# A group of seven in the first feed-forward and packed score products, in a conformer trunk on one Trainium2 core

## Chip, core and metric

The kernel runs on one core of one Trainium2 chip. The metric is the device time of one launch in microseconds (us). Engines are named as the profile names them: PE is TensorE (PEld its weight loads), DVE VectorE, ACT ScalarE, POOL GpSimd, SP SyncE, whose queue issues most of the DMAs.

## The reference

A trunk of two layers over 256 positions of width 1024, all in float32. Cut to what matters here:

```python
def swiglu_ffn(h, w1, w3, w2):                       # D_FF = 2816
    return (silu(h @ w1) * (h @ w3)) @ w2

for i in range(2):
    h = h + 0.5 * swiglu_ffn(rmsnorm(h, ffn_norm1[i]), ffn1_w1[i], ffn1_w3[i], ffn1_w2[i])
    m = rmsnorm(h, mix_norm[i])
    h = h + (conv_module(m, ...) if i == 0 else mla(m, positions, ...))
    h = h + 0.5 * swiglu_ffn(rmsnorm(h, ffn_norm2[i]), ffn2_w1[i], ffn2_w3[i], ffn2_w2[i])
return rmsnorm(h, final_norm)
```

In `mla` (8 heads) a score is the sum of two products, one over 128 unrotated components and one over 64 rotated ones, with one rotated key for all heads:

```python
q_rope, k_rope = apply_rope(q_rope, cos, sin), apply_rope(k_rope, cos, sin)   # angles from positions
for blk in range(2):                                 # query blocks of 128
    s = (einsum("bqhd,bkhd->bhqk", q_nope[:, q0:q1], k_nope[:, :q1])
         + einsum("bqhr,bkr->bhqk", q_rope[:, q0:q1], k_rope[:, :q1])) * scale
    p = softmax(where(chunk mask, s, -inf))
    o = einsum("bhqk,bkhd->bqhd", p, v[:, :q1])
```

## The kernel before

Weights come as blocks of 1 MB (128 x 2048 numbers) on SP's queue into four `raw` buffers. A block is split in two halves of 1024 columns: ACT casts it to a high part of type fp32r, DVE subtracts that from the raw numbers and keeps the low part (`load`, L246 and L247). High and low parts lie in five pairs of buffers. Activations are split in the same way (`Xh`, `Xl`), and `mm3` makes each product of three fp32r matmuls: low by high, high by high, high by low (L332, L335, L336).

A feed-forward has six chunks c of its hidden columns, each of four blocks, the last one of two. A plain block gives 24 matmuls with 512 columns. In `SEVEN_UP` stand the chunks that are worked as a *group of seven*: the four blocks are taken as a two-by-two matrix of blocks, and seven products of sums (12 matmuls each) take the place of four plain blocks of 24. `load_seven` fetches the four raws, makes sums of them in place on DVE (L200, 128 x 2048) and splits the seven results; `whole_rows` adds the activations' two parts to one tile `xs`, which takes a `raw` buffer; `sums_of_rows` and `forms_of` make four sums of it and split these; `seven_products` issues the products. The feed-forwards 1, 2 and 3 do this for chunk 3, and all four do it for part of the down product (`SEVEN_DOWN`). The feed-forwards are numbered 0 to 3; the convolution stands between 0 and 1, the attention between 2 and 3.

The gate rows of a chunk are turned by way of DRAM (`gt`, `gd`, `gb`) and split on ACT and DVE into `Gh` and `Gl` (L853). `diagonals` is a generator for work off the path that `beside()` advances. `rope_tables` makes sines and cosines of the positions; it stands in the program ahead of `mla`, and the scheduler has its DVE part in the first feed-forward, among L1366 to L1391.

In the attention `scores` puts for each head and each query block one fp32 product of `QN` and `KN` (L1584) and one of `QR` and `KR` (L1585) into the same bank. `QR` and `KR` hold the turned part of a head on one half of the partitions; rows of the other half carry the chunk mask as a product. `softmax`, `probs`, `values` and `evicted` follow, and `nope` makes the unrotated queries of heads 4 to 7 in between.

A scheduler sets the order on each engine by its own estimate of times; `order(a, b)` forces a behind b, and `urgent` gives an instruction priority.

Of the kernel before, what the change touches and what calls it, by code (L numbers as in the profile page):

```python
# [19 lines left out]
P = 128  # L20
D = 1024
S = 256
# [25 lines left out]

SEVEN_UP = {1: (3,), 2: (3,), 3: (3,)}
SEVEN_DOWN = (0, 1, 2, 3)  # L50
# [39 lines left out]
def trunk(ctx: ExitStack, tc: tile.TileContext, x, xt, first, pos, invf, gfin, wdw,  # L90
# [72 lines left out]

    casts = {}

    turns = []
# [22 lines left out]
    def load_seven(j, four, b, pieces):  # L189
# [14 lines left out]
        if j == 1:  # L204
            sub(b[11], b[12], b[11])
            sub(b[12], b[22], b[12])
        elif j == 2:
            sub(b[11], b[22], b[11])
        elif j == 6:
            sub(b[11], b[21], b[11])  # L210
# [126 lines left out]

    def sums_of_rows(x11, x12, x21, x22):


        sums = [(0, x22, x21, x22, ALU.add), (2, x21, x11, x21, ALU.subtract), (1, x11, x22, x11, ALU.subtract),
                (3, x12, x12, x11, ALU.subtract)]
        for n, out, left, right, op in sums:
            nc.vector.tensor_tensor(out, left, right, op=op)
# [23 lines left out]
    def seven_products(xh, xl, forms, banks, late={}):  # L368
# [21 lines left out]
        kept = tmp.tile([P, 512], F32, tag="s", name=uid("p5"))  # L390
        last = urgent(nc.scalar.copy)(kept, c22)
        product(forms[1], c21, False)
        add = urgent(nc.vector.tensor_add)(c12, c21, kept)
        order(casts[n0 + 5, 0][1], add.ins)
        for high, low in gates[-NT:] if not late else ():
            order(high, last.ins)
            order(low, add.ins)
        low_gates = [low for high, low in gates[-NT:] if not late]
        product(rows(1, 0), c11, False)
        product(forms[2], c21, False)  # L400
        add = urgent(nc.vector.tensor_add)(c22, c21, kept)
        order(casts[n0 + 6, 0][1], add.ins)
        for low in low_gates[1:]:
            order(low, casts[n0 + 6, PIECES - 1][1].ins)
        product(forms[3], c12, False)
# [247 lines left out]
    class Plain:  # L653
# [9 lines left out]
        @urgent  # L663
        def half(self, tb, i):
            sq = squares(self.ss[tb], h[tb], D, i)
            if tb == 0 and i == 1:
                self.sq = sq

                nc.scalar.activation(small.tile([P, 1], F32, tag="silu", name="sigm"), self.ss[0][:, 1:], AF.Sigmoid)

# [171 lines left out]
    def ffn_in(act, X, make_next, beside, apart, seven_up, seven_down):  # L842
        first_form = {}
        Gh = act.tile([P, NF, S], F32R, tag="Gh", name=uid("Gh"))
# [10 lines left out]
        def first_chunk(X, u):  # L855
# [13 lines left out]
            for n, (m, tb, ks) in enumerate(groups):  # L869
# [12 lines left out]
                last = mm  # L882

        for c in range(6):

# [4 lines left out]
            if c == 0 and X.pool:  # L890
                first_chunk(X, u)
            if seven_up and c == min(seven_up) - (1 if X.whole else 2):
                forms = forms_of(sums_of_rows(*whole_rows(X.xh, X.xl)), Gh[:, 14:], Gl[:, 14:])
            if c in seven_up:
# [4 lines left out]
                beside()  # L899
            if both and seven_down:  # L900
                z11, z21, z12, z22 = (rows4[:, n, :] for n in range(4))
                down_sums = sums_of_rows(z11, z12, z21, z22)
                first_form = forms_of(down_sums[:1], *(act.tile([P, 2, S], F32R, tag=tag, name=uid(tag))
                                                       for tag in ("s1h", "s1l")))
            for m in range(0 if u else 1 if both else 2):
# [453 lines left out]

    def rope_tables():  # L1360
        pi = const.tile([P, NT], I32, name="pi")
# [3 lines left out]
        pf = const.tile([P, NT], F32, name="pf")  # L1365
        nc.vector.tensor_copy(pf, pi)  # L1366
        ang = const.tile([P, NT, 32], F32, name="ang")
# [31 lines left out]
        nc.scalar.activation(sn[:, :, 0, :], r3, AF.Sin, scale=-1.0)  # L1399
        nc.scalar.activation(sn[:, :, 1, :], r3, AF.Sin)  # L1400
        return cc, sn

    def rope(pool, dst, src, n, cc, sn, tb, after=()):

        w = n * 64
        t1, t2 = (pool.tile([P, w], F32, tag=f"rp{w}", name=uid("rp"), bufs=3 if n > 1 else 4) for _ in range(2))
        a = t1[:, :w].rearrange("p (n i f) -> p n i f", i=2, f=32)
# [16 lines left out]
    def mla_in(act, X, make_next, cc, sn):  # L1424
# [6 lines left out]

        KR = act.tile([P, 2, S], F32, tag="KR", name="KR")
        QR = act.tile([P, 2, H // 2, S], F32, tag="QR", name="QR")
        for x, fill in ((KR, -1e30), (QR, 1.0)):
            nc.gpsimd.memset(x, 0.0)
            for parity in range(2):
                for tb in range(NT):
                    row = 64 * (1 - parity) + 32 * tb
                    t = tb * P + (CHUNK if x is KR else 0)
                    nc.gpsimd.memset(x[row:row + 1, parity, ..., t:t + CHUNK], fill)  # L1440

# [123 lines left out]
        (hi, lo), = weights()  # L1565
        for tb in range(NT):
            for d in range(2):
                b = bank("A", "v")
                for k in range(2):
                    c = slice(k * D + d * 512, k * D + d * 512 + 512)  # L1570
                    mm3(b, CKh[:, k, tbs(tb)], CKl[:, k, tbs(tb)], hi[:, c], lo[:, c], k == 0, k == 1)
                kept = nc.scalar.copy(VV[:, tb, d * 512:(d + 1) * 512], b)
# [3 lines left out]

        score_last, maxima, powers, scaled = [], [], [], []

        def scores(hd):
            b = bank("B", "sc")  # L1580
            sc = {0: b[:, :P], 1: b[:, P:P + S]}
            for qb in range(NT):
                n = (qb + 1) * P
                nc.tensor.matmul(sc[qb], QN[:, hd, tbs(qb)], KN[:, hd, :n], start=True, stop=False)  # L1584
                last = nc.tensor.matmul(sc[qb], QR[:, hd % 2, hd // 2, tbs(qb)], KR[:, hd % 2, :n], start=False,  # L1585
                                        stop=True)
            score_last.append(last)
# [21 lines left out]
        def probs(pr):  # L1609
            b = transposed(pr, 0, 3)  # L1610
            pt = act.tile([P, 3 * P], F32, tag="ptT", name=uid("ptT"), bufs=2)
            nc.scalar.copy(pt, b[:, :3 * P])
            return pt

        def evicted(hd, b):
            nc.scalar.copy(Oh[:, hd, :], b[:, :S])
            nc.vector.tensor_sub(Ol[:, hd, :], b[:, :S], Oh[:, hd, :].bitcast(F32))

        def values(hd, pt):
# [3 lines left out]

            (urgent if hd in (3, 4, 5, 6) else lambda f: f)(evicted)(hd, b)

# [4 lines left out]
        table = urgent(nc.scalar.activation)(small.tile([P, 1], F32, tag="silu", name="exp"), neghalf, AF.Exp)  # L1630
        order(table, kept.ins)
        pr[0] = scores(0)
        pr[1] = scores(1)
        pr[2] = scores(2)

        for j, i, highs, lows in ((0, 0, None, maxima[2]), (0, 1, None, scaled[0]), (1, 0, powers[2], scaled[1]),
                                  (1, 1, powers[2], scaled[2])):
            for cast, first in zip(casts[n_used[0] + j, i], (highs, lows)):
                if first is not None:
                    order(cast, first.ins)  # L1640
        nope(part, QN, 4, CQh, CQl, 512, 4, (0, 4), score_last[-1:])
        o = Rows(Oh, Ol, H)
        for i in range(2, H + 3):
# [6 lines left out]
            if i - 2 < H:  # L1650
                pt[i - 2] = probs(pr[i - 2])
            if i - 3 in pt:
                values(i - 3, pt[i - 3])
# [17 lines left out]
    def diagonals():  # L1671
# [5 lines left out]
        for g in (1, 0):  # L1677
            for j in range(KP - g):
                nc.scalar.activation(dpair[g][:, j, :], ident2, AF.Copy, scale=wp2[:, g, j:j + 1])
# [17 lines left out]

    stage = []
    todo = diagonals()

# [13 lines left out]
    X = ffn(X, lambda act: Norm("mix_1", turn_by_dma=rows), apart=True)  # L1714
    cc, sn = rope_tables()
    X = mla(X, lambda act: Norm("ffn2_1", half=True, turn_by_dma=rows), cc, sn)
# [102 lines left out]
```

## Time and profile before

| | |
|---|---|
| median of three runs | 896.05 us (895.89 to 896.4) |
| profiled execution | 896.07 us, span 894.3 us |
| granted TensorE clock | 0.999 |
| busy: PE, DVE, ACT, POOL | 99%, 83%, 64%, 12% of the span |
| DMA | 198.94 MB, 222 GB/s over the span |

The profile is one execution; starts are microseconds from the start of its span. A line of a timeline gives start, duration, engine, line, operation, output and inputs, and behind them in brackets how long the engine had been idle and what it waited for. `x24` means so many instructions in a row. TensorE's durations overlap, so its pace is read from starts. Feed-forward 0 runs to about 182 us, its chunk 3 from 71.5 us on; the scores begin at 666.3 us.

### The profile page before, as it was taken

How to read it: one execution, taken by the hardware profiler on the slowest of the kernel's cores; microseconds unless marked ns; L12 is line 12 of the kernel's file. 1: busy time of each engine (PE TensorE's matmuls, PEld its weight loads, DVE VectorE, ACT ScalarE, POOL GpSimd, SP SyncE). 2: the span in 40 equal slices, each digit the busy share in tenths (PEclk: the TensorE clock that was granted, in tenths of full speed). 3: DMA queues.
4: the chain of work that ended last, by engine and by line, in shares of the span. 5: the costliest groups of instructions: out<-in, count | busy, mean ns of one | idle time of the engine just before them, and what ended most of it. 6: DMA issues, size and time to landing. Idle time of an engine off the chain costs nothing.

```text
span 894.3 us, 12241 instructions
## 1 busy us (share of the span) xinstructions
PE 886.9 (99%) x4221; PEld 745.9 (83%) x4221; DVE 743.1 (83%) x1083; ACT 571.8 (64%) x993; POOL 104.2 (12%) x227
## 2 busy tenths in 40 slices
PE   9999999999999999999999999999999999999997
PEld 7888888898988888888888888888899888888886
DVE  6787789579998999999588989995768579989973
ACT  7966458488886646667375566673677566474752
POOL 1000000069962000000010000001400010000000
PEclk9999999999999999999999999999999999999999
DMA  9987629834215864939759369495635349378541
GB/s 330 375 303 274 232 59 355 295 121 172 106 60 194 289 258 144 374 109 388 259 175 339 118 218 357 123 392 182 223 142 189 141 154 342 104 260 317 180 196 48
DMA packets 71055, 198.94 MB, mean 222 GB/s; under 512 B 12369, under 2 KB 41937, under 8 KB 51665
## 3 DMA queue, kind: packets, MB, share of 16 engines
q1 hardware_dynamic: 70560, 197.47, 61.8%
q8 instruction: 33, 0.54, 0.2%
q10 hardware_dynamic: 432, 0.69, 0.2%
q14 instruction: 30, 0.24, 0.1%
HBM read 181.87 MB, written 16.25 MB: 222 GB/s over the span
## 4 chain that ended last, share of the span: by engine, by line
PE 92%; DVE 4%; ACT 2%; DMA 1%; issue 0%; SPq 0%; POOL 0%; DVEq 0%; ACTq 0%
PE u L336 16%; PE u L335 16%; PE u L332 16%; PE o L335 9%; PE o L336 9%; PE o L332 9%; PE gate L1005 2%; PE u L411 2%; DVE acc L1094 2%; PE u L1005 2%; PE tp L446 1%; PE a L335 1%; PE a L332 1%; PE a L336 1%; PE nope L336 1%; PE nope L332 1%
## 5 line engine op out<-in xcount | busy, mean ns | idle before, releaser
L247 DVE TENSOR_TENSOR lo<-raw,hi 128x1024 fp32r<-128x1024 f32 (+1 forms) x236 | 276.2, 1212 | 38.8 <-ACT hi L246 37.6
L246 ACT CAST hi<-raw 128x1024 fp32r<-128x1024 f32 (+1 forms) x238 | 236.8, 1044 | 89.3 <-DMA raw<-in_f2w 30.8
L332 PE MATMUL u<-lo,Xh 128*128 128x512 f32 x612 | 238.4, 389 | 0.1
L336 PE MATMUL u<-hi,Xl 128*128 128x512 f32 x612 | 238.3, 389 | 0.0
L335 PE MATMUL u<-hi,Xh 128*128 128x512 f32 x612 | 238.1, 389 | 0.0
L332 PEld LDWEIGHTS u<-lo,Xh 128*128 128x128 f32 x612 | 114.9, 188 | 24.5 <-ACT Xh L598 0.5
L336 PEld LDWEIGHTS u<-hi,Xl 128*128 128x128 f32 x612 | 114.9, 188 | 24.3 <-DVE Xl L465 0.5
L335 PEld LDWEIGHTS u<-hi,Xh 128*128 128x128 f32 x612 | 114.9, 188 | 23.8
L214 ACT CAST hi<-raw 128x1024 fp32r<-128x1024 f32 x98 | 97.7, 1050 | 51.8 <-DVE raw L200 44.9
L200 DVE TENSOR_TENSOR lo<-raw,hi 128x1024 fp32r<-128x1024 f32 x98 | 115.6, 1216 | 7.1 <-ACT hi L214 7.1
L332 PE MATMUL o<-lo,Gh 128*128 128x512 f32 (+1 forms) x276 | 106.6, 386 | 0.0
L335 PE MATMUL o<-hi,Gh 128*128 128x512 f32 (+1 forms) x276 | 106.5, 386 | 0.0
L336 PE MATMUL o<-hi,Gl 128*128 128x512 f32 (+1 forms) x276 | 106.5, 386 | 0.0
L437 POOL TENSOR_TENSOR ms<-ss 128x1 f32<-128x1 f32 x16 | 8.1, 510 | 597.6 <-ACT junk L429 597.6
L200 DVE TENSOR_TENSOR raw<-raw,raw 128x2048 f32<-128x2048 f32 x28 | 63.9, 2283 | 1.8 <-DMA raw<-in_f2w 0.9
L332 PEld LDWEIGHTS o<-lo,Gh 128*128 128x128 f32 x276 | 51.8, 188 | 10.5
L335 PEld LDWEIGHTS o<-hi,Gh 128*128 128x128 f32 x276 | 51.9, 188 | 10.5
L336 PEld LDWEIGHTS o<-hi,Gl 128*128 128x128 f32 x276 | 51.8, 188 | 10.4
L1094 DVE SCALAR_TENSOR_TENSOR acc<-V,dw,acc 128x128 f32<-128x128 f32 (+1 forms) x174 | 53.9, 391 | 0.0
L1115 ACT ACTIVATE prod<-V,dw 128x128 f32<-128x128 f32 (+1 forms) x128 | 45.6, 415 | 1.8 <-POOL Y L1116 1.0
L956 ACT ACTIVATE s<-u,R 128x512 f32<-128x512 f32 (+1 forms) x48 | 30.9, 647 | 24.8 <-PE u L336 24.1
L797 DVE SCALAR_TENSOR_TENSOR h<-o,rh,h 128x512 f32<-128x512 f32 (+1 forms) x18 | 12.9, 719 | 29.2 <-PE o L336 29.2
(265 smaller groups left out, 1257.7 us busy)
## 6 DMA issues: line engine op xcount, KB each, us to landing
raw<-in_f2w SPq DMA_DIRECT2D x66, 1024.0 KB, 6.2
raw<-in_f1w SPq DMA_DIRECT2D x62, 1024.0 KB, 6.5
raw<-in_cw SPq DMA_DIRECT2D x12, 1024.0 KB, 5.5
gd<-gt SPq DMA_DIRECT2D x160, 64.0 KB, 3.0
gb<-gd SPq DMA_DIRECT2D x24, 256.0 KB, 2.8
rows<-gd SPq DMA_DIRECT2D x16, 256.0 KB, 4.4
raw<-in_wo SPq DMA_DIRECT2D x4, 1024.0 KB, 4.9
hd<-rows SPq DMA_DIRECT2D x56, 64.0 KB, 2.4
```

What stands on the lines that cost most here:

```text
L200: ins = nc.vector.tensor_sub(out, left, right)
L214: casts[n, i] = nc.scalar.copy(hi[:, c], raw[:, c]), sub(lo[:, c], raw[:, c], hi[:, c].bitcast(F32))
L246: casts[len(loaded), i] = (nc.scalar.copy(hi[:, c], raw[:, c]), low.tensor_sub(lo[:, c], raw[:, c], hi[:, c].bitcast(F32)))
L247: low.tensor_sub(lo[:, c], raw[:, c], hi[:, c].bitcast(F32)))
L332: mm = nc.tensor.matmul(o, ah, bl, start=start, stop=False, skip_group_check=seeded)
L335: nc.tensor.matmul(o, ah, bh, start=False, stop=False, skip_group_check=seeded)
L336: return nc.tensor.matmul(o, al, bh, start=False, stop=stop, skip_group_check=seeded)
L411: mm = nc.tensor.matmul(o, al if kind == "x" else ah, bl if kind == "l" else bh, start=start and n == 0, stop=stop and n == len(kinds) - 1)
L956: nc.scalar.activation(s[:, :w], u[0, tb][:, :w], AF.Silu, scale=X.r[tb])
L1005: mm = nc.tensor.matmul(u[:, t], w[:, c], X.x[:, k, t], start=(k == 0), stop=(k == KT - 1))
L1094: dve_last.append(nc.vector.scalar_tensor_tensor(out if j == j1 - 1 else y, v, w, y, op0=ALU.mult, op1=ALU.add))
L1115: prods_last.append(nc.scalar.activation(p, v, AF.Copy, scale=w))
```

## The change

1. Chunk 3 of feed-forward 0 becomes a group of seven, like those of the other three. For all four the sums of the activations are now made two chunks ahead (before: two, or one where the feed-forward takes its input whole), behind the sixth block's low part in feed-forward 0. The sums for the group of the down product are made a little earlier in the program.
2. The turned part of the scores is made of two fp32r products. `KA` holds the high part of the turned key on both halves of the partitions, `QA` the low part of a query on one half and its high part on the other; `QR` holds the high part of the query and the mask's ones, `KR` the low part of the key and the mask. So `QA` by `KA` gives low by high and high by high, `QR` by `KR` high by low. For the second query block these two come ahead of `QN` by `KN`.
3. In `seven_products` the last two gate rows' splits stand behind the next plain block's parts, and the two before them behind one of the sums of raws.
4. `rope_tables` is made at the end of `diagonals`, so later in feed-forward 0, and the table load for the sigmoid of the convolution stands behind its last sine.
5. Around the softmax some casts of weights are put behind other instructions than before, and the eviction of head 2 gets priority too.

```diff
-SEVEN_UP = {1: (3,), 2: (3,), 3: (3,)}
+SEVEN_UP = {0: (3,), 1: (3,), 2: (3,), 3: (3,)}
...
-    def whole_rows(xh, xl):
+    def whole_rows(xh, xl, after=()):
         x = rawp.tile([P, HB], F32, tag="raw", name=uid("xs")).rearrange("p (k t) -> p k t", t=S)
-        nc.vector.tensor_add(x, xh.bitcast(F32), xl.bitcast(F32))
+        whole = nc.vector.tensor_add(x, xh.bitcast(F32), xl.bitcast(F32))
+        for a in after:
+            order(whole, a.ins)
...
+        for high, low in gates[-2 * NT:-NT] if not late else ():
+            order(low, thirds[n0 + 2].ins)
+        late_gates = []
         for high, low in gates[-NT:] if not late else ():
-            order(high, last.ins)
-            order(low, add.ins)
-        low_gates = [low for high, low in gates[-NT:] if not late]
+            late_gates.append((high, low))
...
-        for low in low_gates[1:]:
-            order(low, casts[n0 + 6, PIECES - 1][1].ins)
+        for n, (high, low) in enumerate(late_gates):
+            order(high, casts[n0 + 5 + n, PIECES - 1][0].ins)
+            order(low, casts[n0 + 7, PIECES - 1][1].ins)
...
-            if seven_up and c == min(seven_up) - (1 if X.whole else 2):
-                forms = forms_of(sums_of_rows(*whole_rows(X.xh, X.xl)), Gh[:, 14:], Gl[:, 14:])
+            if seven_up and c == min(seven_up) - 2:
+                after = [casts[5, PIECES - 1][1]] if X.whole else ()
+                forms = forms_of(sums_of_rows(*whole_rows(X.xh, X.xl, after)), Gh[:, 14:], Gl[:, 14:])
...
+            nc.scalar.copy(KA[:, tbs(t)], b[:, :P])
             for i in range(2):
                 half = slice(64 * i, 64 * i + 64)
-                nc.scalar.copy(KR[half, i, tbs(t)], b[half, :P])
+                nc.vector.tensor_sub(KR[half, i, tbs(t)], b[half, :P], KA[half, tbs(t)].bitcast(F32))
+        turns_of = [], []
         for tb in range(NT):
-            b = transposed(qr[tb], 0, 4, (last,)).rearrange("p (j t) -> p j t", t=P)
-            for parity, copy in ((0, nc.scalar.copy), (1, nc.vector.tensor_copy)):
-                half = slice(64 * parity, 64 * parity + 64)
-                urgent(copy)(QR[half, parity, :, tbs(tb)], b[half])
+            b = transposed(qr[tb], 0, 4, (last,), turns_of[tb]).rearrange("p (j t) -> p j t", t=P)
+            for parity in range(2):
+                half, rest = (slice(64 * i, 64 * i + 64) for i in (parity, 1 - parity))
+                high = QR[half, parity, :, tbs(tb)]
+                turned_last = urgent(nc.scalar.copy)(high, b[half])
+                both = act.tile([P, 512], F32R, tag="rp512", name=uid("QA"), bufs=6).rearrange("p (j t) -> p j t", t=P)
+                urgent(nc.vector.tensor_sub)(both[rest], b[half], high.bitcast(F32))
+                urgent(nc.vector.tensor_copy)(both[half], high)
+                QA[parity, tb] = both
...
                 n = (qb + 1) * P
-                nc.tensor.matmul(sc[qb], QN[:, hd, tbs(qb)], KN[:, hd, :n], start=True, stop=False)
-                last = nc.tensor.matmul(sc[qb], QR[:, hd % 2, hd // 2, tbs(qb)], KR[:, hd % 2, :n], start=False,
-                                        stop=True)
+                three = [(QN[:, hd, tbs(qb)], KN[:, hd, :n]), (QA[hd % 2, qb][:, hd // 2], KA[:, :n]),
+                         (QR[:, hd % 2, hd // 2, tbs(qb)], KR[:, hd % 2, :n])]
+                for i, (rows_of, keys) in enumerate(three if qb == 0 else three[1:] + three[:1]):
+                    mm = nc.tensor.matmul(sc[qb], rows_of, keys, start=i == 0, stop=i == 2)
+                    if last is not None:
+                        order(mm, last.ins)
+                    last = mm
...
         nc.scalar.activation(ident2, ident2, AF.Copy, scale=wp2[:, 1, KP - 1:])
+        yield
+        tables.extend(rope_tables(casts[n_used[0] + 1, PIECES - 1][1]))
```

How this moves instructions is seen in three places. PE's queue in the attention, from the first scores on, before:

```order
L1584 MATMUL sc_6245<-KN,QN 128x128
L1585 MATMUL sc_6245<-KR,QR 128x128
L1584 MATMUL sc_6245<-KN,QN 128x256
L1584 MATMUL sc_6261<-KN,QN 128x128
L1585 MATMUL sc_6261<-KR,QR 128x128
L1584 MATMUL sc_6261<-KN,QN 128x256
L1585 MATMUL sc_6245<-KR,QR 128x256
L1585 MATMUL sc_6261<-KR,QR 128x256
```

The same place after; `QA_6161` and `QA_6174` are the packed queries of the even heads for the two query blocks, `QA_6165` those of the odd heads for the first:

```order
L1614 MATMUL sc_6289<-KN,QN 128x128
L1614 MATMUL sc_6289<-KA,QA_6161 128x128
L1614 MATMUL sc_6289<-KR,QR 128x128
L1614 MATMUL sc_6307<-KN,QN 128x128
L1614 MATMUL sc_6307<-KA,QA_6165 128x128
L1614 MATMUL sc_6307<-KR,QR 128x128
L1614 MATMUL sc_6289<-KA,QA_6174 128x256
L1614 MATMUL sc_6289<-KR,QR 128x256
L1614 MATMUL sc_6289<-KN,QN 128x256
```

A head has six matmuls where it had four, and the first one on a packed query of the second block stands seventh.

SP's queue in feed-forward 0, from the end of the first loads on, before (`raw_380` is the fourth block of chunk 1):

```order
L238 DMA raw_380<-in_f1w 128x2048
L238 DMA raw_388<-in_f1w 128x2048
L482 DMA gd_359<-gt_357 32x4x128 x4
L238 DMA raw_453<-in_f1w 128x2048
L482 DMA gd_372<-gt_370 32x4x128 x4
```

After, where `raw_394` is that block, and the buffer that held `raw_380` is taken by `xs_380`, which no DMA fills:

```order
L489 DMA gd_359<-gt_357 32x4x128 x4
L239 DMA raw_394<-in_f1w 128x2048
L494 DMA rows_139<-gd_359 128x512
L239 DMA raw_402<-in_f1w 128x2048
L489 DMA gd_372<-gt_370 32x4x128 x4
```

Two fetches of weights that stood ahead of the first turned rows now stand behind them.

DVE's queue in feed-forward 0 around chunk 3, before (`s_689` and `s_703` are the gate rows of chunk 2, `lo_719` and `lo_727` blocks at the end of chunk 3 and the start of chunk 4):

```order
L247 TENSOR_TENSOR lo_719<-raw_717,hi_718 128x1024 x2
L853 TENSOR_TENSOR Gl_185<-rows_139,Gh_184 128x4x128
L958 TENSOR_TENSOR s_689<-s_689,u_635 128x512
L344 TENSOR_TENSOR rows_139<-rows_139 128x512
L478 STREAM_TRANSPOSE gt_692<-s_689 128x512
L958 TENSOR_TENSOR s_703<-s_703,u_636 128x512
L344 TENSOR_TENSOR rows_139<-rows_139 128x512
L247 TENSOR_TENSOR lo_727<-raw_725,hi_726 128x1024
```

After, from the second gate rows of chunk 2 (`s_722`) to the first plain block of chunk 4 (`lo_819`); `lo_741`, `lo_760`, `lo_780` and `lo_799` are the low parts of the group's last four products:

```order
L201 TENSOR_TENSOR lo_741<-raw_647,hi_740 128x1024 x2
L201 TENSOR_TENSOR lo_760<-raw_575,hi_759 128x1024 x2
L259 TENSOR_TENSOR u_739<-u_737,p_106_777 128x512
L201 TENSOR_TENSOR lo_780<-raw_637,hi_779 128x1024
L201 TENSOR_TENSOR raw_573<-raw_647,raw_573 128x2048
L201 TENSOR_TENSOR lo_780<-raw_637,hi_779 128x1024
L259 TENSOR_TENSOR u_738<-u_737,p_106_777 128x512
L201 TENSOR_TENSOR lo_799<-raw_573,hi_798 128x1024 x2
L259 TENSOR_TENSOR s_886<-s_886,u_739 128x512
L248 TENSOR_TENSOR lo_819<-raw_817,hi_818 128x1024 x2
```

Ahead of these ten rows stand the two gate rows, the third product's low part `lo_646` in two halves, and two transposes. The sums for the down product (L344) have left this place for a later one, and the gates of chunk 2 (`Gl`) follow behind `lo_819`.

More of the change, by code (lines that the diff above doesn't have):

```diff
@@ L882, in first_chunk, with down @@
                 last = mm
+        def down():
+            z11, z21, z12, z22 = (rows4[:, n, :] for n in range(4))
+            down_sums.extend(sums_of_rows(z11, z12, z21, z22, casts[n_used[0], 0][1] if X.whole else None))
+            first_form.update(forms_of(down_sums[:1], *(act.tile([P, 2, S], F32R, tag=tag, name=uid(tag))
+                                                        for tag in ("s1h", "s1l"))))
         for c in range(6):
@@ L1611, in probs @@
             pt = act.tile([P, 3 * P], F32, tag="ptT", name=uid("ptT"), bufs=2)
[L1612 removed]
+            copies.append(nc.scalar.copy(pt, b[:, :3 * P]))
             return pt
         def evicted(hd, b):
[L1616 to L1617 removed]
+            kept = (nc.scalar.copy(Oh[:, hd, :], b[:, :S]),
+                    nc.vector.tensor_sub(Ol[:, hd, :], b[:, :S], Oh[:, hd, :].bitcast(F32)))
+            if hd in (1, 2, 3):
+                for i in range(PIECES):
+                    for cast, first in zip(casts[len(loaded) - (2 if hd == 1 else 1), i], kept):
+                        order(cast, first.ins)
         def values(hd, pt):
@@ L1634, in mla_in @@
         pr[2] = scores(2)
[L1636 to L1640, printed above, removed]
+        for j, i, lows in ((0, 0, maxima[2]), (0, 1, scaled[0]), (1, 0, scaled[1]), (1, 1, scaled[2])):
+            high, low = casts[n_used[0] + j, i]
+            order(low, lows.ins)
+            if j == 1:
+                late.append(high)
         nope(part, QN, 4, CQh, CQl, 512, 4, (0, 4), score_last[-1:])
@@ L1651, in mla_in @@
                 pt[i - 2] = probs(pr[i - 2])
+            if i < 4:
+                order(late[i - 2], copies[-1].ins)
             if i - 3 in pt:
```

58 lines of the change are left out of this document (33 added, 25 removed).

## Prediction

> **What bounds the kernel now.** I read the page first: the busy times and the chain that ended last.
>
> ```profile
> PE 886.9 (99%) x4221; PEld 745.9 (83%) x4221; DVE 743.1 (83%) x1083; ACT 571.8 (64%) x993; POOL 104.2 (12%) x227
> PE 92%; DVE 4%; ACT 2%; DMA 1%; issue 0%; SPq 0%; POOL 0%; DVEq 0%; ACTq 0%
> ```
>
> TensorE is busy through the whole span, but a busy TensorE may be waiting inside its own pipeline, so I asked next for its waits and for its pace. The waits of PE are two rows:
>
> ```profile
> PE warm L324 <- DVE still L319: 1.0, 1, 1.0
> PE u L411 <- ACT Xh L640: 0.2, 1, 0.2
> ```
>
> Both lie ahead of the eighth microsecond. The pace is read from starts in PE's timeline, here at the end of the first feed-forward:
>
> ```profile
> 174.18 0.39 PE L332 MATMUL o<-lo,Gh 128*128 128x512 f32 x1
> ...
> 181.43 0.39 PE L336 MATMUL o<-hi,Gl 128*128 128x512 f32 x1
> ```
>
> These are the first and last of 33 rows, so one 512-column matmul takes 7.25/32 = 0.2266 us. The duration in the second column, 0.39, overlaps the next one and must not be added up. So at present every matmul taken away is worth its pace, as long as its operands still come in time. What is left for them to be late by is read from the stages:
>
> ```profile
> core 0: us, PE busy (x) PEld busy (x) DVE busy (x) ACT busy (x) POOL busy (x), PEclk, DMA share, GB/s
> 0.00:104.00 104.00, 102.77 (x453) 84.06 (x454) 76.42 (x107) 71.80 (x127) 3.79 (x19) 1.00 0.88 316
> 104.00:182.00 78.00, 78.00 (x348) 64.60 (x347) 60.59 (x60) 49.18 (x80) 0.95 (x3) 1.00 0.61 222
> 290.00:410.00 120.00, 120.00 (x531) 99.34 (x530) 113.07 (x117) 73.45 (x90) 0.00 (x0) 1.00 0.69 245
> ```
>
> The third row holds the second feed-forward's group of seven: DVE is busy 113 of 120 us there and PE still never waits. The first feed-forward (first row) has 27.6 us of idle DVE, but its DMA engines are busy 88% of the time.
>
> **The group in the first feed-forward.** Four blocks of 24 matmuls become seven products of 12: 96 − 84 = 12 matmuls fewer, 12 × 0.2266 = **−2.72 us** if all operands are in time. PE enters this chunk at 71.50 and would leave it 84 × 0.2266 = 19.03 us later, at 90.53. What is added is on DVE and ACT; prices from the page and DVE's timeline:
>
> ```profile
> L200 DVE TENSOR_TENSOR raw<-raw,raw 128x2048 f32<-128x2048 f32 x28 | 63.9, 2283 | 1.8 <-DMA raw<-in_f2w 0.9
> 32.47 2.35 DVE L247 TENSOR_TENSOR lo<-raw,hi 128x1024 fp32r<-128x1024 f32 x2
> ...
> 41.02 0.20 DVE L1391 TENSOR_SCALAR red_abs<-red_abs 128x64 f32<-128x64 f32 x1
> 41.18 2.36 DVE L247 TENSOR_TENSOR lo<-raw,hi 128x1024 fp32r<-128x1024 f32 x2
> 70.87 0.69 DVE L344 TENSOR_TENSOR rows<-rows 128x512 f32<-128x512 f32 x1
> 71.47 0.70 DVE L478 STREAM_TRANSPOSE gt<-s 128x512 f32<-128x512 f32 x1
> ```
>
> DVE gains four raw subtractions (9.1 us), three more blocks' low halves (7.1), the whole rows (2.3, same size as a raw subtraction), four sums and four low forms (8 × 0.69 = 5.5): 24 us before PE's 91st. It loses the rope tables: between 34.7 and 41.2 all but two low halves (2 × 1.18) are rope's, some 4.1 us. Net 20 us against 27.6 idle, so it fits on the whole, and the question is the last part. Order has ScalarE and DVE finish c = 2's gate rows (s_722) only once PE is through c = 2, at 71.7. From there to lo_819, the next plain block, stand twelve low halves (14.2 us), one raw subtraction (2.3), five 512-column operations (3.4) and two transposes (1.4): 21.3 us by durations. Each overlaps its follower by about 0.08 (the x2 row takes 2.36, two single ones 2.44), and s_708 runs before 71.7: 19 us by pace. So lo_819's second half lands between 90.8 and 92.3; PE wants it six matmuls in, at 91.9. Counting back 3.0 us (lo_819 and s_886) gives the last product's second half at 87.8 to 89.3, wanted at 89.2; the earlier products are further ahead. I take no wait, and 0.4 us at worst.
>
> What the whole rows cost before that is a raw buffer: xs_380 takes the buffer that block four of c = 1 has now, and that block is fetched into the next one to come free, behind the first transposed rows on SP's queue.
>
> ```profile
> 21.13 7.65 SPq L238 DMA_DIRECT2D raw<-in_f1w  x2
> 29.07 2.17 SPq L482 DMA_DIRECT2D gd<-gt  x4
> 37.39 1.22 DVE L247 TENSOR_TENSOR lo<-raw,hi 128x1024 fp32r<-128x1024 f32 x1
> ```
>
> Its fetch goes from 21.1 to about 31.3. With the page's median 6.5 us to landing and 2.2 for the first cast and low half it is usable near 40.2; PE wants it at 27.98 + 3 × 24 × 0.2266 = 44.3. Slack shrinks but stays.
>
> **The scores.** Eight heads, two query blocks each; the turned part is now two fp32r matmuls in place of one fp32.
>
> ```profile
> L1585 PE MATMUL sc<-KR,QR 128*128 128x256 f32 x16 | 4.6, 379 | 0.0
> L1585 PE MATMUL sc<-KR,QR 128*128 128x128 f32 x16 | 3.1, 275 | 0.0
> 668.96 0.38 PE L1584 MATMUL sc<-KN,QN 128*128 128x128 f32 x2
> 669.18 0.39 PE L1585 MATMUL sc<-KR,QR 128*128 128x128 f32 x2
> 669.40 0.60 PE L1584 MATMUL sc<-KN,QN 128*128 128x256 f32 x2
> 669.83 0.59 PE L1585 MATMUL sc<-KR,QR 128*128 128x256 f32 x2
> ```
>
> x16 for eight heads and x2 in the timeline: one fp32 matmul runs as two passes. From start to start the 128-column pair takes 0.22, the 256-column pair 0.43. The fp32r price at 256 columns stands in the nope products, and the nearest rows to fp32r at 128 columns are the transposes:
>
> ```profile
> 649.07 0.28 PE L335 MATMUL nope<-CQ,hi 128*128 128x256 f32 x1
> 649.19 0.28 PE L336 MATMUL nope<-CQ,lo 128*128 128x256 f32 x1
> 181.82 0.87 PE tp L446 x8
> ```
>
> 0.12 for 256 columns; 0.87/8 = 0.109 for a 128-column single pass. No row shows fp32r at 128 columns, so it lies between 0.06 (half of the 256-column one, if nothing but columns counts) and 0.22 (the fp32 price). I take 0.115, by the transposes, which also load 128 weight columns each. Per head: 0.22 + 0.43 = 0.65 goes, 2 × 0.12 + 2 × 0.115 = 0.47 comes: 0.18 × 8 = **−1.44 us**. The ends: −2.3 at 0.06, +0.24 at 0.22.
>
> The Trainium skill, "TensorE: Matmul & The Clock Gate", section "Back-to-back issue gap", quotes about 81 ns for a 128-column and 131 ns for a 512-column matmul in a stream. By its 81 the term would be an estimated −2.0. The 512-column pace of this trace, 227 ns, disagrees with that page's 131, so I leave its 81 out of the sum too.
>
> The new operands are split on DVE and ACT. DVE has four subtractions and four copies of 64x512 where it had two copies, ACT four casts for two:
>
> ```profile
> 661.25 0.69 DVE L258 COPY QR<-tp 64x512 f32<-64x512 f32 x1 [1.90 <-ACT QR L258]
> 665.80 0.69 DVE L258 COPY QR<-tp 64x512 f32<-64x512 f32 x1 [3.86 <-ACT QR L258]
> 668.73 1.15 DVE L1597 TENSOR_REDUCE nm<-sc 128x1 f32<-128x128 f32 x4 [2.23 <-PE sc L1585]
> ```
>
> 8 × 0.69 = 5.5 us from 660.6 on, with the second tile's transposes pinned three products earlier: the four packed tiles are done near 662.4, 664.2, 665.3 and 666.4. The scores start at 666.3, want the first at once, and the last only behind two heads' work at 669. It fits, with the idle 2.23 in front of the first maximum as further cover. Without that cover it would cost up to 2 us.
>
> **The rest.** The gate splits of the other three groups go behind the next plain block: its low half comes earlier, but PE did not wait for it, so 0; if a split (0.69) came too late for the down products, 3 × 0.69 = 2.1 us. The rope tables move to DVE's idle stretches near 165 to 176 and its sines on ACT ahead of the sigmoid's table load: hidden, see below.
>
> **Sum.** −2.72 − 1.44 = −4.16 on the profiled execution's 896.07 gives 891.91; its span of 894.3 becomes 890.1, with the same 1.8 us around it. The runs' median is 896.05, so no correction: **891.9 us**. A measurement of this kernel tells about 0.2%, 1.8 us, from no change.
>
> **Rivals.**
> - *Operands late by a little* (0.17): the group's last low halves, or the exponentials of heads 1 and 2, which ACT now does behind a copy of the second nope products, come one to two microseconds late; the score term is eaten. 896.07 − 2.72 = 893.3. For it: the 0.4 above. Against: the 113 of 120 us without a wait.
> - *fp32r at 128 columns costs as fp32* (0.08): −2.72 + 0.24, 893.6.
> - *Only columns count* (0.04): 0.06 apiece, −2.72 − 2.3, 891.0; the transposes speak against it. The skill's 81 ns would lie on this side.
> - *The rope tables sit on the path into the convolution* (0.10). They stand between the last low halves and the residual adds:
>
> ```profile
> 173.43 2.36 DVE L247 TENSOR_TENSOR lo<-raw,hi 128x1024 fp32r<-128x1024 f32 x2 [3.08 <-ACT hi L246]
> 177.78 0.75 DVE L797 SCALAR_TENSOR_TENSOR h<-o,rh,h 128x512 f32<-128x512 f32 x1 [1.33 <-PE o L336]
> 180.53 0.49 DVE L679 TENSOR_SCALAR hn<-h,R 128x512 f32<-128x512 f32 x1 [2.00 <-POOL R L440]
> ```
>
>   hn is the row the transposes wait for, and ends 0.4 to 0.6 us before them. If none of the 4.1 us fell into the 3.08 us gaps, the transposes would start 3.6 us later: 895.5, no change that could be told. It decides from 0.5 us of delay on. Against: two such gaps and the 1.33 before the second add.
> - *Three raw buffers starve the first feed-forward* (0.08), the slower case. While xs_380 holds its buffer, to about 50 us, the other three carry six blocks. A buffer's round now runs from its issue (28.8, the second of the 7.65 row) to its last low half (43.5, the row at 41.18): 14.8 us, a third of which is 4.9, under PE's 5.44 per block. From a round of 16.3 us PE waits. If the whole rows, sums and forms (7.8) came on top in full, 22.6/3 = 7.5 per block: 6 × 2.1 − 4.4 of lead = 8.2 us lost, 900.1. Against: landing, cast and low half need only 6.5 + 2.0 + 2.4 = 10.9 of the 14.8, the rest is waiting for a turn, and rope's 4.1 leave this stretch.
>
> **Chances and range.** The forecast itself has 0.53; with the three small rivals faster by over 0.2% (below 894.26) has 0.82; within 0.2% is rope's 0.10; slower 0.08. The range starts below the 891.0 case by the pace's own error (0.2) at 890.8, and reaches past the late operands and the dear 128 columns, 893.6, by the 0.4 of the group and 0.7 for a split, to 894.7. The rope and buffer cases stay outside, 0.18.
>
> **What would show it.** Right: 84 matmuls between the group's first start and the next chunk's, 19.0 us apart; no new row among PE's waits; heads 0.18 us shorter. Wrong: a PE wait on DVE lo near 87 to 92 us or on raw before 60; starts of KA,QA at 128 columns 0.22 apart; tp <- hn later than the last o product at about 179; PE waiting for ptT or Oh near 676 to 680.

## The result and the profile after

| | before | after |
|---|---|---|
| median | 897.31 us (six runs, 895.89 to 900.12) | 892.47 us (six runs, 892.40 to 893.54) |
| ratio, 95% interval | | 0.9951 (0.994 to 0.9962) |
| profiled execution | 896.07 us, span 894.3 | 893.54 us, span 891.8 |

The change makes the kernel 0.5% faster: 0.0049 of the time before is 4.4 us, by the interval 3.4 to 5.4. The forecast was 891.9 us and 4.16 us. The profiled execution is the longest of the six after, by 0.8 us, and its span is only 2.5 us shorter than that of before; the profile of before took 896.07 us, and three of its six runs 898.2 to 900.1. So the sum seems to have come out, but where each microsecond went has to be read from the traces. Busy times and chain of after, from the page:

```profile
PE 883.5 (99%) x4209; PEld 742.5 (83%) x4209; DVE 769.5 (86%) x1114; ACT 579.6 (65%) x1005; POOL 104.9 (12%) x227
PE 91%; DVE 5%; DMA 2%; ACT 1%; issue 1%; POOL 0%; DVEq 0%; ACTq 0%; SPq 0%
```

PE lost 3.4 us of busy time, DVE gained 26.4. PE's waits, two rows before, are now these (total, times, longest):

```profile
PE warm L325 <- DVE still L320: 1.0, 1, 1.0
PE o L333 <- DVE lo L201: 0.6, 2, 0.4
PE rb L1165 <- POOL rc L1161: 0.4, 1, 0.4
PE o L337 <- DVE rows L369: 0.2, 1, 0.2
```

The group itself, first matmul and first matmul of the next chunk in PE's timeline:

```profile
71.14 0.39 PE L333 MATMUL u<-lo,Xh 128*128 128x512 f32 x1
...
90.18 0.39 PE L333 MATMUL u<-lo,Xh 128*128 128x512 f32 x1
```

90.18 − 71.14 = 19.04 us, 84 matmuls at 0.2267: no wait inside it. The loss is further on, in the group of the same feed-forward's down product:

```profile
133.50 0.39 PE L337 MATMUL o<-hi,Gl 128*128 128x512 f32 x1
133.86 0.50 PE L333 MATMUL o<-lo,rows 128*128 128x512 f32 x1
...
136.48 0.39 PE L337 MATMUL o<-hi,rows 128*128 128x512 f32 x1
137.28 0.47 PE L333 MATMUL o<-lo,rows 128*128 128x512 f32 x1 [0.41 <-DVE lo L201]
```

From start to start 0.36 and 0.80 where the pace is 0.23, and a few slow matmuls behind. To see what this costs, each matmul is paired with the same one in the profile before ("matched rows" from here on). PE is 0.36 us earlier already ahead of the group, from its first microseconds; four profiles of the changed kernel are 0.2 to 0.7 earlier there, others with parts of the change from 0.8 earlier to 0.2 later, so this is taken as chance. It is 3.05 to 3.08 us earlier behind the group, as 12 × 0.2266 = 2.72 more should make it, and 2.05 earlier from 141 us on: 1.0 us is given back here. Why is seen in the windows of DVE, before and then after:

```profile
core 0: us, DVE busy (x), PEclk, DMA share, GB/s
80.00:100.00 20.00, 11.61 (x14) 1.00 0.77 279
100.00:120.00 20.00, 17.53 (x16) 1.00 0.33 120
120.00:140.00 20.00, 15.55 (x17) 1.00 0.42 119
```

```profile
80.00:100.00 20.00, 20.00 (x22) 1.00 0.91 358
100.00:120.00 20.00, 20.00 (x22) 1.00 0.73 266
120.00:140.00 20.00, 19.84 (x22) 1.00 0.47 153
```

DVE had 15.3 us of idle time in these 60 us, now 0.16. So the late low halves waited for their turn on DVE, and DVE hardly ever for a DMA or another engine.

The scores of one head, after, stand between two other products:

```profile
676.98 0.39 PE L1614 MATMUL sc<-KN,QN 128*128 128x128 f32 x2
677.12 0.31 PE L1614 MATMUL sc<-KA,QA 128*128 128x128 f32 x1
677.26 0.27 PE L1614 MATMUL sc<-KR,QR 128*128 128x128 f32 x1
677.38 0.33 PE L1614 MATMUL sc<-KA,QA 128*128 128x256 f32 x1
677.54 0.28 PE L1614 MATMUL sc<-KR,QR 128*128 128x256 f32 x1
677.66 0.59 PE L1614 MATMUL sc<-KN,QN 128*128 128x256 f32 x2
678.10 0.49 PE L453 MATMUL tp<-ident,pr 128*128 128x128 f32 x3
```

678.10 − 676.98 = 1.12 us for a head. The same head before:

```profile
678.64 0.39 PE L1584 MATMUL sc<-KN,QN 128*128 128x128 f32 x2
...
679.95 0.49 PE L446 MATMUL tp<-ident,pr 128*128 128x128 f32 x3
```

1.31 us. (`QN` by `KN` for the first block shows 0.14 us to the next start where it showed 0.22 before, since the first packed matmul starts 0.03 us behind its second pass; the head as a whole is the surer measure.) Matched rows give 1.63 us over all eight heads: PE is 0.87 us earlier than before where the scores begin, 2.50 behind them.

That PE is only 0.87 us earlier at the scores comes of two more places: 0.7 us at `rb`, in the convolution, and 1.0 us between 570 and 581 us, in the third feed-forward's down group. (Near 286 us it gains 0.4, where the profile of before alone has a slow spot.) At 570 to 581 us PE's waits are again on DVE, 0.20 us on `rows` and 0.17 on `lo`.

### The profile page after: what moved, and what is told of

Read it like the earlier page. It is cut to its first block, busy times and chain, and to the rows that moved or that the text cites. A ratio compares the mean times of both kernels' runs of the same rounds, so it can differ in the third digit from the quotient of the medians.

```text
span 891.8 us, 12296 instructions
## 1 busy us (share of the span) xinstructions
PE 883.5 (99%) x4209; PEld 742.5 (83%) x4209; DVE 769.5 (86%) x1114; ACT 579.6 (65%) x1005; POOL 104.9 (12%) x227
## 4 chain that ended last, share of the span: by engine, by line
PE 91%; DVE 5%; DMA 2%; ACT 1%; issue 1%; POOL 0%; DVEq 0%; ACTq 0%; SPq 0%
PE u L333 15%; PE u L336 15%; PE u L337 15%; PE o L333 8%; PE o L337 8%; PE o L336 8%; PE u L1019 3%; PE gate L1019 3%; PE u L418 2%; PE o L1255 2%; DVE lo L201 2%; DMA raw<-in_f1w 2%; DVE raw L201 1%; PE sc L1614 1%; PE tp L453 1%; PE pairs L1062 1%
## 5 line engine op out<-in xcount | busy, mean ns | idle before, releaser
L248 DVE TENSOR_TENSOR lo<-raw,hi 128x1024 fp32r<-128x1024 f32 (+1 forms) x228 | 266.6, 1208 | 27.2 <-ACT hi L247 26.5
L247 ACT CAST hi<-raw 128x1024 fp32r<-128x1024 f32 (+1 forms) x230 | 228.3, 1044 | 69.4 <-DMA raw<-in_f2w 24.2
L337 PE MATMUL u<-hi,Xl 128*128 128x512 f32 x592 | 230.4, 389 | 0.0
L336 PE MATMUL u<-hi,Xh 128*128 128x512 f32 x592 | 230.3, 389 | 0.0
L333 PE MATMUL u<-lo,Xh 128*128 128x512 f32 x592 | 230.2, 389 | 0.0
L215 ACT CAST hi<-raw 128x1024 fp32r<-128x1024 f32 x112 | 111.6, 1050 | 54.3 <-DVE raw L201 48.3
L201 DVE TENSOR_TENSOR lo<-raw,hi 128x1024 fp32r<-128x1024 f32 x112 | 131.8, 1213 | 6.4 <-ACT hi L215 6.1
L337 PEld LDWEIGHTS u<-hi,Xl 128*128 128x128 f32 x592 | 111.1, 188 | 23.5 <-DVE Xl L472 0.5
L333 PEld LDWEIGHTS u<-lo,Xh 128*128 128x128 f32 x592 | 111.1, 188 | 23.1
L201 DVE TENSOR_TENSOR raw<-raw,raw 128x2048 f32<-128x2048 f32 x32 | 73.1, 2284 | 0.5
```

What stands on the lines that cost most here:

```text
L201: ins = nc.vector.tensor_sub(out, left, right)
L215: casts[n, i] = nc.scalar.copy(hi[:, c], raw[:, c]), sub(lo[:, c], raw[:, c], hi[:, c].bitcast(F32))
L247: casts[len(loaded), i] = (nc.scalar.copy(hi[:, c], raw[:, c]), low.tensor_sub(lo[:, c], raw[:, c], hi[:, c].bitcast(F32)))
L248: low.tensor_sub(lo[:, c], raw[:, c], hi[:, c].bitcast(F32)))
L333: mm = nc.tensor.matmul(o, ah, bl, start=start, stop=False, skip_group_check=seeded)
L336: nc.tensor.matmul(o, ah, bh, start=False, stop=False, skip_group_check=seeded)
```

## The experiments

Each experiment was timed beside the kernel before and beside a repeat of the changed kernel, its control: 892.73 us for the first three, 892.90 for the two with GpSimd and for the group without packed scores, 892.14 for the rest. The medians of the three controls differ by up to 0.8 us, so a difference is always taken to the control beside it. Differences below are of medians unless a trace is named.

**The changed kernel again** (three times). Expected of the first:

> The changed kernel itself, profiled once more. Theory (A): PE got 2.7 us of matmuls fewer in the first feed-forward, but from 80 us to 150 us DVE now has no idle time, so the group of the down product there gets its low halves late and PE gives back about 1 us near 134 to 137 us; a second give-back of about 1 us near 571 to 579 us comes from weights and row buffers that keep their own time there. If both are the kernel's own, a second profile shows both again within 0.3 us. Rival (B): they are chance, of DMA landings, and the five unprofiled runs, 1 us shorter than the profiled one, are the kernel as it is: then at least one of the two is gone in this profile. Time about 0.9951 of before.

of the others:

> The changed kernel again, as the control of this call: waits of 1 us in all near 134 to 137 us, as in both profiles so far.

> The changed kernel again, control of this call: 0.4 us of PE waits on DVE lo near 137 us.

Measured: 892.73, 892.90 and 892.14 us; ratios 0.9955 (0.994 to 0.9971), 0.996 (0.9945 to 0.9975), 0.9945 (0.9928 to 0.9961). PE's wait on DVE in the down group is in all of them; the row of the first and of the third:

```profile
137.80 0.47 PE L333 MATMUL o<-lo,rows 128*128 128x512 f32 x1 [0.36 <-DVE lo L201]
```

```profile
137.14 0.47 PE L333 MATMUL o<-lo,rows 128*128 128x512 f32 x1 [0.41 <-DVE lo L201]
```

The wait at `rb` is in all three as well. The loss between 570 and 581 us is in none of them. The first has one of 0.7 us elsewhere (PE `a` on ACT `Xh`, at 625 us), and in matched rows 0.4 us near 90 us: there the low half of the next plain block waits 0.45 us for ACT's cast, and that cast 1.36 for a fetch of weights. The two others have no further loss of that size. So the loss at 134 to 137 us is the kernel's own, as theory A said, and the one at 570 to 581 comes and goes, as the rival said; half of each was right.

**Without the packed scores.** The turned part is one fp32 product again:

```diff
-three = [(QN.., KN..), (QA.., KA..), (QR.., KR..)]
+two = [(QN.., KN..), (QR.., KR..)]          # QR, KR fp32, copied as before
```

> Only the packed score products are undone: the turned part is one fp32 product again, with its two copies, all else as changed. The prediction's price for the packed products, 0.18 us a head, says 1.44 us longer than the changed kernel (the trace after reads 1.31 to 1.12 us per head, 1.5 us). If a wait in the softmax ate it, less; if a 128-column fp32r matmul cost as fp32, 0.2 us shorter.

Measured: 893.85 us, 1.12 above the control. Matched rows: PE is 1.95 us earlier than in the profile after where the scores begin and 0.45 behind them, so the scores take 1.5 us more. The packed products are worth their price in the trace; the medians show 1.1. The profile of this kernel lacks the wait at `rb`, 0.7 us, which all four of the changed kernel have; if its other executions lack it too, that makes up the difference.

**Without the first feed-forward's group.**

```diff
-SEVEN_UP = {0: (3,), 1: (3,), 2: (3,), 3: (3,)}
+SEVEN_UP = {1: (3,), 2: (3,), 3: (3,)}
```

> Only the first feed-forward's chunk 3 goes back to four plain blocks; packed scores, gate order and the place of the rope tables stay as changed. If the group brings its full twelve matmuls: 2.7 us longer than the changed kernel. Theory A (DVE full behind the group, 1 us given back in the down product): 1.7 us longer, and PE has no wait near 134 to 140 us. If the group's DVE work cost all it saves: no difference.

Measured: 894.11 us, 1.38 above the control, and one PE wait in all, the 1.0 us at the program's start (so the wait at `rb` is not in this profile either). PE is 2.51 us later than after at chunk 4, but only 1.48 from 141 us on; 0.2 us earlier ahead of the group, it lacks the whole 2.72. The group brings its twelve matmuls and gives 1.0 us back in the down product.

**The gate splits in their old order.**

```diff
-for high, low in gates[-2 * NT:-NT]: order(low, thirds[n0 + 2].ins)
-for n, (high, low) in enumerate(late_gates): order(high, casts[n0 + 5 + n, 1][0].ins); order(low, casts[n0 + 7, 1][1].ins)
+for high, low in gates[-NT:]: order(high, last.ins); order(low, add.ins)     # and the second low behind casts[n0 + 6, 1]
```

> Only the order of the gate splits in the groups goes back to that of before; all else as changed. The prediction gives this part nothing: within 0.3 us of the changed kernel. If the later splits hold row buffers that the transfers of turned rows wait for, and so the weights behind them on SP's queue, then the wait near 571 to 579 us is theirs and this kernel is up to 1 us shorter. If they were needed for the new group in the first feed-forward, where DVE is full, the split in front of the next plain block makes this kernel 0.7 to 1.4 us longer.

Measured: 894.13 us, 1.40 above the control, as the third case said. Its waits of PE:

```profile
PE u L333 <- ACT u L259: 1.2, 1, 1.2
PE warm L325 <- DVE still L320: 1.0, 1, 1.0
PE u L333 <- DVE lo L201: 0.9, 1, 0.9
PE o L333 <- DVE lo L201: 0.6, 2, 0.4
```

The first is in the new group, at 77.6 us. How it comes about is seen on DVE, in this kernel:

```profile
66.25 0.68 DVE L860 TENSOR_TENSOR Gl<-rows,Gh 128x512 fp32r<-128x512 f32 x1
69.23 0.69 DVE L860 TENSOR_TENSOR Gl<-rows,Gh 128x512 fp32r<-128x512 f32 x1 [2.30 <-ACT Gh L860]
69.84 2.28 DVE L201 TENSOR_TENSOR raw<-raw,raw 128x2048 f32<-128x2048 f32 x1
```

and in the changed one:

```profile
65.74 2.29 DVE L201 TENSOR_TENSOR raw<-raw,raw 128x2048 f32<-128x2048 f32 x1
67.95 1.28 DVE L862 TENSOR_TENSOR Gl<-rows,Gh 128x512 fp32r<-128x512 f32 x2
```

A low part at the head of DVE's queue waits 2.30 us for its high part, and ACT has waited 2.46 for the turned rows to land before it makes that; the sum of raws behind it starts 4.1 us later. ACT's cast of that sum, and behind it the copy of the first product that PE needs, come late in turn (72.22 in place of 68.21 us, 76.97 in place of 74.11). In the changed kernel ACT waits as long for the same rows, 2.55 us, but there the sum stands ahead of those low parts. Putting those two low parts behind the sum is one of the two moves of the new order; the 0.9 us at 357 us is in the second feed-forward.

**The group without packed scores and with the old gate order.**

> The first feed-forward's group without the packed scores and with the gate splits' old order. By single terms: 1.1 to 1.5 us above the changed kernel for the scores and 1.4 us for the gates, so 2.5 to 2.9 us above the control; of the group's 2.7 us hardly 1 us is then left beside before. If the gate order matters only with the scores' or other shifts, it is 1.3 us above.

Measured: 896.37 us, ratio 0.9995 (0.9985 to 1.0004): not to be told from before, and 3.5 above the control, more than the single terms add up to. So the group by itself, with the gates as they stood, is worth nothing that can be measured. The traces say the same of the first feed-forward alone: from just ahead of the group to 160 us PE gains 1.3 to 1.7 us on before in the four profiles of the changed kernel, and loses 0.2 and 0.3 in the two that have the group with the old gate order.

**The packed scores with neither group nor new gate order.**

> Of the change the packed scores with what was moved around them, but neither the group in the first feed-forward nor the new order of the gate splits. With the scores alone at 1.44 us: 1.4 us under before. The kernel with the new gate order and without the group was 2.4 us under before; if the gate order is worth something to the other three groups too, this one is above that by it; if it is needed by the new group only, the two are the same.

Measured: 895.04 us, 1.58 under before; ratio 0.9982 (0.997 to 0.9993). With the new gate order (the kernel without the group, above) the ratio was 0.997 (0.9959 to 0.9982). The intervals overlap, so whether the gate order helps the other three groups by itself stays open; the difference, each to the kernel before beside it, is 0.8 us.

**Low parts on GpSimd.** To relieve DVE where it is full:

```diff
-low = nc.gpsimd if len(loaded) == conv_block[-4] else nc.vector
+low = nc.gpsimd if len(loaded) in (conv_block[-4], 21, 23) else nc.vector
```

> The changed kernel, but the low parts of two plain blocks of the first feed-forward (the third of chunk 4 and the first of chunk 5) are subtracted on GpSimd, which is idle there: 4.6 us of DVE work leave the stretch between 90 and 115 us. DMAs, buffers and PE's matmuls stay. Theory (DVE full from 80 to 150 us makes the down group's low halves late): PE's waits near 134 to 137 us go and about 1 us comes back, against the control of this call. Rival (late DMAs, or the third raw buffer held by the whole rows): the waits stay, no difference. If GpSimd takes 2.4 us for a half, as it does in the convolution, and slows DVE beside it, or a block comes late for PE at 101 or 112 us, it is longer.

Measured: 897.26 us, 4.4 above the control. GpSimd's timeline, and beside it DVE's:

```profile
94.20 12.40 POOL L248 TENSOR_TENSOR lo<-raw,hi 128x1024 fp32r<-128x1024 f32 x4 [70.21 <-DVE lo L248]
```

```profile
97.96 6.39 DVE L248 TENSOR_TENSOR lo<-raw,hi 128x1024 fp32r<-128x1024 f32 x2 [1.31 <-ACT hi L247]
104.27 4.33 DVE L345 TENSOR_TENSOR rows<-rows 128x512 f32<-128x512 f32 x3
```

Two low halves take 6.39 us on DVE where they take 2.35, three row sums 4.33 where they take 2.05: DVE loses 6.3 us to save 4.6, and PE waits 3.5 us in two places (127.3 and 132.3 us) ahead of the late low halves. Instruction by instruction the two engines are seen to take turns:

```profile
97.52 2.41 POOL L248 TENSOR_TENSOR lo<-raw,hi 128x1024 fp32r<-128x1024 f32 x1
97.96 3.06 DVE L248 TENSOR_TENSOR lo<-raw,hi 128x1024 fp32r<-128x1024 f32 x1 [1.31 <-ACT hi L247]
99.90 3.36 POOL L248 TENSOR_TENSOR lo<-raw,hi 128x1024 fp32r<-128x1024 f32 x1
100.94 3.40 DVE L248 TENSOR_TENSOR lo<-raw,hi 128x1024 fp32r<-128x1024 f32 x1
```

GpSimd's first row ends at 99.93, DVE's 1.09 us later; GpSimd's next ends 2.24 us behind that, at 103.26, and DVE's next 1.08 behind that. These are a little under the times that each takes alone, 1.2 and 2.37, so each got on only once the other was through. Of the three row sums only the first, under GpSimd's last half, is longer: 2.88 us, the two behind it 0.69 each. The experiment cannot acquit or convict DVE's load, since it made it larger. With the same in all feed-forwards:

> The same two blocks' low parts on GpSimd in all four feed-forwards. If the waits that come and go near 571 to 579 us are DVE's too, another 0.5 to 1 us comes back beside the kernel with only the first; if they are those of DMA landings, nothing more.

Measured: 907.66 us, ratio 1.0122 (1.01 to 1.0143), and PE waits 4.8 us on low parts of plain blocks alone. It said nothing on the waits near 571 us.

**Two low parts left out**, so that DVE gets its relief and no engine gets the work:

```diff
-low.tensor_sub(lo[:, c], raw[:, c], hi[:, c])
+low.tensor_sub(lo[:, d], raw[:, d], hi[:, d])      # d: 32 of 1024 columns in blocks 21 and 23; their matmuls read hi for lo
```

> The changed kernel, in which two blocks of the first feed-forward (the third of chunk 4 and the first of chunk 5) have no low part: all but 32 columns of each half's subtraction are left out and their matmuls read the high part in its place, so the numbers differ and the matmuls stay. 4.6 us of DVE work leave the stretch from 90 to 115 us and nothing comes onto another engine. Theory (DVE full from 80 to 150 us): PE's waits near 134 to 137 us go and 1 us comes back against the control. Rival (DMA landings or the third raw buffer): waits and time as the control.

Measured: 891.66 us, 0.5 under the control's 892.14. All waits of PE in its profile:

```profile
PE warm L327 <- DVE still L322: 1.0, 1, 1.0
```

Against the control's profile PE is 0.30 us earlier ahead of the two places, as it was from the start, and 1.36 behind them: the down group's 1.0 us is back. The same DMAs are issued and the whole rows hold the same buffer, so it was DVE's load, as DVE's 0.16 us of idle time said. (The wait at `rb` is gone too, which makes the profile another 0.7 us shorter.) The medians give half a microsecond in all; the five runs lie in two groups, two at 890.4 and three at 891.7 to 891.9, and tell no more.

**The remedy that keeps the result.** The splits of chunk 3's gates, which stand ahead of the late low parts, go behind the down group:

```diff
+for gate in gates[-3 * NT:-2 * NT] if X.whole else ():
+    for ins, cast in zip(gate, casts[n_used[0] - 1, PIECES - 1]): order(ins, cast.ins)
```

> The changed kernel with the gate splits of the first feed-forward's chunk 3 also put behind the group of the down product: 2 x 0.65 us of DVE work go from ahead of the late low parts to behind them. Theory: about 1 us less waiting near 134 to 137 us, a kernel faster than both, unless the row buffers that these splits hold longer keep transfers, and the weights behind them on SP's queue, waiting after 140 us. Rival: no difference.

Measured: 893.16 us, 1.0 above the control. The wait at 137 us stays, and another comes, 0.5 us on DVE for a low part of a plain block: matched rows lose 0.8 us between 142 and 153 us. DVE is full behind the group as well, and what is put off is only paid later. (This profile loses another 0.9 us at 396 to 407 us, in the second feed-forward's down group, like the first one after at 570 to 581; it is the longest of its six executions.) No version here that keeps the result beats the changed kernel.

## Why the prediction was right, and where its steps were not

- **The bound.** Right: PE's matmuls set the time. That 4.16 us fewer of them came so near the measured 4.4 us (3.4 to 5.4) is in part luck, as the sum at the end of this section shows.
- **The group's matmuls.** Right to 0.01 us: 19.04 us for 84, no wait among them. The last low halves, put at 0 to 0.4 us late, were not late in three of the four profiles of the changed kernel; in the fourth the next chunk lost 0.4 us behind a late fetch of weights.
- **"Net 20 us against 27.6 idle, so it fits on the whole."** This is the step that failed. The 27.6 us were DVE's idle time from 0 to 104 us, and I ended the walk at 91.9 us. The same window after, in the columns of the windows above; DVE had 76.42 before:

```profile
0.00:104.00 104.00, 91.33 (x101) 1.00 0.80 292
```

  By 104 us DVE has done 14.9 us more than before, not 20. The rest runs on behind it, and the down group's row sums, which stood at 70 to 78 us, now follow there too, at 101 to 111 us. DVE is full from 80 to 150 us, and the first product that pays is in the down group at 134 to 137 us: 1.0 us in the four profiles of the changed kernel, gone in the one with 4.6 us less DVE work. The rival of operands that come a little late had the kind of loss and its size, but looked for it at the group's end and in the softmax. The term was 2.7 − 1.0 = 1.7 us, and the medians gave 1.4.
- **The whole rows' buffer.** Right: the fourth block of chunk 1 is split here, and PE asks for it only at 43.94 us:

```profile
37.20 2.36 DVE L248 TENSOR_TENSOR lo<-raw,hi 128x1024 fp32r<-128x1024 f32 x2
```

  Ready at 39.6, where 40.2 was expected; the rival of the three buffers did not come.
- **The scores.** Right: 0.19 us a head against 0.18, and 1.5 to 1.65 us over the eight in the traces against 1.44. The pair of 128-column matmuls runs 0.14 and 0.12 from start to start, a little over the 0.115 taken, and each far from fp32's 0.22 and from 0.06. The estimate by "TensorE: Matmul & The Clock Gate" of the Trainium skill (81 ns, section "Back-to-back issue gap") lies too low here. No wait was seen in the softmax.
- **"The gate splits: 0."** Wrong. Undone in the changed kernel, they cost 1.4 us. The prediction asked what the move would gain in the three old groups, where PE did not wait, and not what the new group would wait for without it. The part that was costed at nothing is what lets the group pay.
- **The rope tables.** Right: hidden. The transposes behind `hn` start as much earlier as the products around them, 2.05 us.
- **Not in the sum at all:** the loss at `rb`, 0.7 us in matched rows, in all four profiles of the changed kernel and not in the one of before. The last section shows where it comes from.

Put together again with what the traces show, 1.7 us for the group, 1.6 for the scores, 0.4 at 286 us and 0.7 lost at `rb`, the sum is 3.0 and the time 893.1 us from the profile before; the median is 892.47, and the controls' are 892.14 to 892.90. The forecast of 891.9 missed by 0.6, less than the microsecond of the down group alone. By the ratios the change is worth more than this sum, 4.4 us and in the controls 3.6 to 4.9. A part of that is the side of before: its profile, from which the forecast and the matched rows start, took 896.07 us, and its medians beside the result and the controls are 896.5 to 897.3. What makes its other executions longer no trace here shows.

## What to carry to other kernels

Idle time is spent where the work lands, not where it is counted: when a change adds work to a second engine, follow its queue from the change until it is idle again, and take the first product beyond as the one that may wait. A reordering that gains nothing in the old kernel can still be the condition of a change beside it, so price each part also with the others in place. And before work is moved to an idle engine, look whether the two share something: here the relief cost more than the load.

## What was not expected of the hardware

A 128x1024 fp32 subtraction on GpSimd and one on VectorE wait for each other: 12.4 us for four halves on GpSimd (3.1 each, 2.37 in the convolution of the kernel before), and 6.39 us for two on VectorE in place of 2.35. The Trainium skill states the contention for VectorE instructions with two SBUF inputs ("GPSIMD Engine Reference", "Key points"); that they took turns, instruction by instruction, is from this trace.

The same accounts for PE's wait at `rb`, though no experiment moved it on purpose. `rc` is a column of 128 numbers that GpSimd makes and PE turns into `rb`. After, and then before:

```profile
257.76 2.35 DVE L248 TENSOR_TENSOR lo<-raw,hi 128x1024 fp32r<-128x1024 f32 x2
259.06 1.47 POOL L1161 TENSOR_TENSOR rc<-msc,neghalf 128x1 f32<-128x1 f32 x1 [1.88 <-ACT msc L1159]
```

```profile
260.17 2.35 DVE L247 TENSOR_TENSOR lo<-raw,hi 128x1024 fp32r<-128x1024 f32 x2
261.11 0.69 POOL L1147 TENSOR_TENSOR rc<-msc,neghalf 128x1 f32<-128x1 f32 x1 [1.83 <-ACT msc L1145]
```

In all fourteen profiles `rc` ends 0.40 to 0.42 us behind the VectorE half under which it begins. Before, it begins 0.94 us behind the start of VectorE's pair, 0.27 us ahead of the end of the first half, and takes 0.69. After, it begins 1.30 us behind that start, just inside the second half, and takes 1.47. PE's wait is in the nine profiles with the long `rc` and in none of the five with the short one. What shifts VectorE's pair against `rc` stays open.
